# Ten elementwise instructions of each attention head move from GpSimd to VectorE and ScalarE

## The chip, the cores and the metric

The program runs on one core of a Trainium2 chip. A core has engines that run side by side, each through its own list of instructions in a fixed order: TensorE (PE in the profile, with PEld for its weight loads) does matmuls, VectorE (DVE) and GpSimd (POOL) do elementwise work on whole tiles, ScalarE (ACT) does functions of one input, and SyncE (SP) starts the loads of weights. An engine waits on semaphores for what another engine has to finish first. The metric is the device time of one execution in microseconds (us), lower is better.

## The reference

The model runs three blocks in turn over 512 tokens of width 1024. The change lies in the first two, which are alike and are called layers here. In each of them, eight groups of columns of one big projection feed two kinds of heads:

```python
for layer in range(DEPTH):            # DEPTH = 2
    h = rmsnorm(x, attn_norm[layer])
    proj = h @ w_in[layer]
    (a_q, a_k, a_v, b_q, b_ff, b_fb, b_i, b_g, gate_a, gate_b) = split_columns(proj)
    y_a = diff_attention(a_q, a_k, a_v, cos, sin, ...) @ w_a[layer]
    y_b = hgrn2_bidirectional(b_q, b_ff, b_fb, b_i, b_g, ...) @ w_b[layer]
    merged = sigmoid(gate_a) * y_a + sigmoid(gate_b) * y_b
    x = x + merged @ w_o[layer]
    ...                               # feed-forward part
```

`diff_attention` has 4 heads: queries and keys are rotated (a product with a cosine table plus a product of the shuffled tile with a sine table), and each head takes the difference of two softmaxes. `hgrn2_bidirectional` has 4 heads too: a linear recurrence over the tokens with a forget gate per channel, run forward and backward and added. Then follow a feed-forward part in each layer and a third block of another kind, which the change does not touch.

## The kernel before

Activations lie with channels on the 128 partitions and the 512 tokens along the free axis, so most tiles are 128x512 in float32. Every weight is loaded as `wraw`, and split into two parts, `whi` by ScalarE (L204) and `wlo` by VectorE (L205), and every projection is three matmuls for one product (L230 to L232). These matmuls are most of TensorE's work everywhere.

Each of the two layers has a heads part (about 88 to 310 us and 917 to 1140 us of the span), which goes through four heads, some 60 us each. A head h consists of

- `proj_rope` for the head's keys and queries: a projection, a shuffle (L650) and two products, one with the cosine table on VectorE (L651) and one with the sine table on GpSimd (L652, tile `rsh`), their sum (L653), and a split of the sum (`stack_split`) into `ak` or `aq` by ScalarE (L239) and VectorE (L243);
- `proj_h`: the projections of the recurrent head, its tiles in `H4` (forward keys, backward queries, forward queries, backward keys), and the sum of the two keys on GpSimd (L687, tile `hks`);
- `attn`, four blocks of queries: scores `at` (L249, L250), maxima (L715), exponentials `e` (L718), the two softmaxes' factors `arc` (L722, L723), their difference (L725), a transpose `tp` on TensorE (L728), and the product with the values (L734);
- `hgrn`, a scheme that doubles the block at each of eight levels (hh = 1, 2, 4, ... 128). A level copies the keys of the halves that it needs into `hKT` (L661, ScalarE), multiplies them with the queries on TensorE (L759; L767 at the last level), writes the result under a mask into `hWd` (L761, VectorE), and then multiplies the left halves (GpSimd from the second level on) and the right halves (VectorE) of all four tiles of `H4` in place with the decay `hT` (both L780). The next level's copy reads what these products wrote. After the last level come transposes of the keys (L793) and the last matmuls (L800 to L812);
- `head_norm`, with its power on GpSimd (L526).

`both` goes through `attn` and `hgrn` in turn, two levels for one block of queries, and the projections of the next head stand behind them in the program. A planner in the framework turns the program into one fixed list of instructions per engine before the launch: it goes through an estimated time, and each engine takes the earliest instruction of the program that the estimate calls ready. So TensorE's list has projections of the next head between the small matmuls of this one. In the run the lists are followed strictly, whatever the real times are.

Of the kernel before, what the change touches and what calls it, by code (L numbers as in the profile page):

```python
# [15 lines left out]
AF = mybir.ActivationFunctionType  # L16
ALU = mybir.AluOpType
# [54 lines left out]
def model_kernel(ctx: ExitStack, tc: tile.TileContext, I, O, dbg=None):  # L72
    nc = tc.nc
    V, A, P, PE = nc.vector, nc.scalar, nc.gpsimd, nc.tensor
# [548 lines left out]
    def heads(l, Win, nrm, oA, oB, op_, ah):  # L623
        Crs = ah.tile([128, 512], F32, name="Crs")
        Srs = ah.tile([128, 512], F32, name="Srs")
# [19 lines left out]
        def proj_rope(c0, tag):  # L645
            mark("proj_" + tag)
            ps = projA(Win, c0, 1, xs)[0]
            t1 = ah.tile([128, 512], F32, name="rt1", tag="rt1", bufs=1)
            sh = ah.tile([128, 512], F32, name="rsh", tag="rsh", bufs=1)
            V.stream_shuffle(out=sh, in_=ps, mask=[(i ^ 8) if i < 16 else i for i in range(32)])  # L650
            V.tensor_tensor(out=t1, in0=ps, in1=Crs, op=ALU.mult)  # L651
            P.tensor_tensor(out=sh, in0=sh, in1=Srs, op=ALU.mult)  # L652
            V.tensor_tensor(out=t1, in0=t1, in1=sh, op=ALU.add)  # L653
            dst = ah.tile([128, 2 if tag == "aq" else 4, 512], F32R, name=tag, tag=tag, bufs=2)
            stack_split(t1, dst)
            return dst
# [7 lines left out]
        def proj_h(h, rest=None):  # L664

            mark(f"projH{h}")
            ps = projA(Win, 1536 + h * 128, 1, xs)[0]
            q = ah.tile([128, 512], F32, name="hq", tag="hq", bufs=1)
            V.tensor_tensor(out=q, in0=ps, in1=rbc, op=ALU.mult)
            H4 = ah.tile([128, 4, 512], F32, name="H4", tag="H4", bufs=2)  # L670
            F2 = ah.tile([128, 2, 512], F32, name="F2", tag="F2", bufs=1)
            for d in range(2):
                ps = projA(Win, 2048 + d * 512 + h * 128, 1, xs)[0]
                z = ah.tile([128, 512], F32, name="hz", tag="hz", bufs=1)
                V.tensor_tensor(out=z, in0=ps, in1=rbc, op=ALU.mult)
                kk = H4[:, 0 if d == 0 else 3, :]
                A.activation(out=F2[:, d, :], in_=z, func=AF.Sigmoid)
                A.activation(out=kk, in_=z, func=AF.Sigmoid, scale=-1.0)
                if l == 1:
                    om = lbc[:, 1, d, h:h + 1]  # L680
                    V.tensor_scalar(out=F2[:, d, :], in0=F2[:, d, :], scalar1=om, scalar2=lbc[:, 0, d, h:h + 1],
                                    op0=ALU.mult, op1=ALU.add)
                    V.tensor_scalar(out=kk, in0=kk, scalar1=om, scalar2=None, op0=ALU.mult)
                V.tensor_tensor(out=H4[:, 2 if d == 0 else 1, :], in0=q, in1=F2[:, d, :], op=ALU.mult)
            KT = left_keys(H4, 1)
            ks = ah.tile([128, 512], F32, name="hks", tag="hks", bufs=1)
            P.tensor_tensor(out=ks, in0=H4[:, 0, :], in1=H4[:, 3, :], op=ALU.add)  # L687
            if rest is not None:
                rest()
                mark(f"projH{h}")  # L690
            dps = hg_ps()
            for b in range(4):
                sl = slice(b * 128, (b + 1) * 128)
                PE.matmul(out=dps[:, sl], lhsT=ks[:, sl], rhs=q[:, sl], start=True, stop=True)
            Wd = ah.tile([128, 4, 128], F32, name="hWd", tag="hWd", bufs=2)
            A.copy(out=Wd.rearrange("p a b -> p (a b)"), in_=dps)
            ps = projA(Win, 3584 + h * 128, 1, xs)[0]
            sg = op_.tile([128, 512], F32, name="hsg", tag="hsg", bufs=3)
            V.tensor_tensor(out=sg, in0=ps, in1=rbc, op=ALU.mult)
            A.activation(out=sg, in_=sg, func=AF.Sigmoid)  # L700
            return H4, F2, Wd, sg, KT
# [42 lines left out]
        def hgrn(h, H4, F2, Wd, sg, KT):  # L744
            T = F2
            W1 = ah.tile([128, 4, 128], F32, name="hW1", tag="hW1", bufs=1)
            kF, qB, qF, kB = (H4[:, i, :] for i in range(4))
            for li, hh in enumerate(LEVELS + [128]):
                nb = 512 // (2 * hh)
                mark(f"hgrn{h}")  # L750
                if hh <= 64:
                    ps = hg_ps()
                    n2 = 64 // hh

                    if li:
                        KT = left_keys(H4, hh)
                    for b in range(4):
                        sl = slice(b * 128, (b + 1) * 128)
                        PE.matmul(out=ps[:, sl].rearrange("p (n two h) -> p n two h", two=2, h=hh), lhsT=KT[:, sl],  # L759
                                  rhs=halves(H4, 1, 2, hh, b * 128, 128), start=True, stop=True)  # L760
                    V.copy_predicated(out=Wd, mask=cm[:, li, :].unsqueeze(1).to_broadcast([128, 4, 128]),  # L761
                                      data=ps.rearrange("p (a b) -> p a b", b=128))
                else:
                    ps = hg_ps()
                    for b in range(4):
                        sl, tl = slice(b * 128, (b + 1) * 128), slice((b ^ 1) * 128, (b ^ 1) * 128 + 128)
                        PE.matmul(out=ps[:, sl], lhsT=(kB if b & 1 else kF)[:, sl], rhs=(qB if b & 1 else qF)[:, tl],  # L767
                                  start=True, stop=True)
                    A.copy(out=W1.rearrange("p a b -> p (a b)"), in_=ps)
                Tv = T.rearrange("p d (n two) -> p d n two", two=2)  # L770
                for half in range(2):
                    v = H4[:, 2 * half:2 * half + 2, :].rearrange("p d (n two h) -> p d n two h", two=2, h=hh)
                    tgt = v[:, :, :, half, :]
                    mul = Tv[:, :, :, 1 - half]
                    eng = P if half == 0 and hh > 1 else V
                    if hh == 1:
                        eng.tensor_tensor(out=tgt.rearrange("p d n h -> p d (n h)"),
                                        in0=tgt.rearrange("p d n h -> p d (n h)"), in1=mul, op=ALU.mult)
                    else:
                        eng.tensor_tensor(out=tgt, in0=tgt, in1=mul.unsqueeze(3).to_broadcast([128, 2, nb, hh]),  # L780
                                        op=ALU.mult)
                if hh < 128:
                    T2 = ah.tile([128, 2, nb], F32, name="hT", tag=f"hT{hh}", bufs=1)
                    V.tensor_tensor(out=T2, in0=Tv[:, :, :, 0], in1=Tv[:, :, :, 1], op=ALU.mult)
                    T = T2
                yield

            mark(f"hgrn{h}")
            vs = slice(h * 128, (h + 1) * 128)
            ps = hg_ps()  # L790
            for b in range(4):
                sl = slice(b * 128, (b + 1) * 128)
                PE.transpose(ps[:, sl], (kB if b > 1 else kF)[:, sl], ident)  # L793
            KT = ah.tile([128, 512], F32, name="hKT", tag="hKT", bufs=1)
            A.copy(out=KT, in_=ps)
            yield
            mark(f"hgrn{h}")
            ps = hg_ps()
            for b in range(4):
                PE.matmul(out=ps[:, b // 2 * 128:b // 2 * 128 + 128], lhsT=KT[:, b * 128:(b + 1) * 128], rhs=vb[:, b, vs],  # L800
                          start=b % 2 == 0, stop=b % 2 == 1)
            St = ah.tile([128, 256], F32, name="hSt", tag="hSt", bufs=1)
            A.copy(out=St, in_=ps[:, 0:256])
            yield
            mark(f"hgrn{h}")
            o = hg_ps()
            for t in range(4):
                tl = slice(t * 128, (t + 1) * 128)
                PE.matmul(out=o[:, tl], lhsT=(qF if t > 1 else qB)[:, tl], rhs=St[:, 0:128] if t > 1 else St[:, 128:256],
                          start=True, stop=False)  # L810
                PE.matmul(out=o[:, tl], lhsT=W1[:, t ^ 1, :], rhs=vb[:, t ^ 1, vs], start=False, stop=False)
                PE.matmul(out=o[:, tl], lhsT=Wd[:, t, :], rhs=vb[:, t, vs], start=False, stop=True)  # L812
            A.copy(out=oB[:, h, :], in_=o)
            yield
# [478 lines left out]
    with ExitStack() as mst:  # L1293
        with ExitStack() as st:
# [63 lines left out]
            for i in range(4):  # L1358
# [3 lines left out]
                                in0=sg[:, i, :].rearrange("p (j n) -> p n j", j=C),  # L1362
# [274 lines left out]
```

## Time and profile before

| | |
|---|---|
| median of 3 runs | 2335.88 us (2334.86 to 2336.14) |
| the profiled execution's own time | 2336.02 us |
| its span, first to last instruction | 2334.2 us |
| TensorE busy | 2295.8 us (98%) |
| VectorE busy | 1354.9 us (58%) |
| ScalarE busy | 1028.1 us (44%) |
| GpSimd busy | 405.3 us (17%) |

The profiled execution's time is its span and 1.8 us around it. Busy time of TensorE is not the same as TensorE at its peak: its matmuls overlap in the records, a 128x512 one is shown with 0.39 us though the next one starts 0.23 us later.

### The profile page before, as it was taken

The numbers are of one execution on the slowest core, as the hardware profiler recorded it, in microseconds if no ns is written. First come the engines' busy times: TensorE is split into PE (matmuls) and PEld (weight loads), VectorE is DVE, ScalarE is ACT, GpSimd is POOL, SyncE is SP. The second block draws the span as 40 slices with busy tenths as digits, with TensorE's granted clock in tenths as the row PEclk, the third lists the DMA queues.
The fourth block names the chain that finished last, engine by engine and source line by source line (L and its number), as shares of the span: only waits on it lengthen the run. The fifth ranks groups of instructions, "written<-read, shape, count | busy, mean of one in ns | idle before, by whom it ended". The sixth has DMA issues, their size and how long they took to land. (4 is left out here: it accounts for less than half of the span.)

```text
span 2334.2 us, 30091 instructions
## 1 busy us (share of the span) xinstructions
PE 2295.8 (98%) x11175; PEld 1908.5 (82%) x11175; DVE 1354.9 (58%) x2368; ACT 1028.1 (44%) x1912; POOL 405.3 (17%) x728
## 2 busy tenths in 40 slices
PE   9999999999999999999999999999999999999998
PEld 7877788888888888787788888888877888888887
DVE  5777755644444556888556444444776875534344
ACT  6566644433233245666533333232457354534232
POOL 1122210070233201222100546020000102000002
PEclk9999999999999999999999999999999999999999
DMA  6211124333333342111143343332443533233331
GB/s 228 72 55 55 55 73 154 102 106 103 115 97 111 107 141 82 55 55 55 55 135 100 101 128 96 111 108 89 125 141 101 177 112 126 91 92 98 100 99 65
DMA packets 241267, 237.40 MB, mean 102 GB/s; under 512 B 18936, under 2 KB 215112, under 8 KB 241120
## 3 DMA queue, kind: packets, MB, share of 16 engines
q1 hardware_dynamic: 221728, 204.81, 28.9%
q10 hardware_dynamic: 15584, 21.33, 2.8%
q0 software_dynamic: 3808, 9.33, 1.3%
q8 instruction: 88, 1.44, 0.3%
q14 instruction: 59, 0.48, 0.1%
HBM read 216.42 MB, written 20.59 MB: 102 GB/s over the span
## 5 line engine op out<-in xcount | busy, mean ns | idle before, releaser
L205 DVE TENSOR_TENSOR wlo<-wraw,whi 128x512 fp32r<-128x512 f32 x736 | 521.0, 713 | 685.5 <-ACT whi L204 677.1
L204 ACT ACTIVATE whi<-wraw 128x512 fp32r<-128x512 f32 x736 | 459.2, 629 | 896.4 <-PE mm L231 675.1
L230 PE MATMUL mm<-xg,whi 128*128 128x512 f32 (+1 forms) x1736 | 677.8, 390 | 0.0
L231 PE MATMUL mm<-xg,whi 128*128 128x512 f32 (+1 forms) x1736 | 675.4, 389 | 0.4 <-DVE xg L1414 0.3
L232 PE MATMUL mm<-xg,wlo 128*128 128x512 f32 (+1 forms) x1736 | 672.8, 388 | 0.0
L230 PEld LDWEIGHTS mm<-xg,whi 128*128 128x128 f32 x1736 | 326.4, 188 | 65.5 <-issue 2.2
L232 PEld LDWEIGHTS mm<-xg,wlo 128*128 128x128 f32 x1736 | 326.3, 188 | 64.7 <-issue 0.8
L231 PEld LDWEIGHTS mm<-xg,whi 128*128 128x128 f32 x1736 | 326.6, 188 | 62.9 <-DVE xg L1414 0.8
L230 PE MATMUL mm<-a,whi 128*128 128x512 f32 x352 | 137.0, 389 | 0.0
L231 PE MATMUL mm<-a,whi 128*128 128x512 f32 x352 | 136.9, 389 | 0.0
L232 PE MATMUL mm<-a,wlo 128*128 128x512 f32 x352 | 136.9, 389 | 0.0
L780 POOL TENSOR_TENSOR H<-H,hT 128x512 f32<-128x512 f32 x56 | 67.2, 1199 | 217.5 <-PE hg L759 122.4
L230 PEld LDWEIGHTS mm<-a,whi 128*128 128x128 f32 x352 | 66.1, 188 | 14.0 <-issue 0.2
L231 PEld LDWEIGHTS mm<-a,whi 128*128 128x128 f32 x352 | 66.1, 188 | 13.7
L232 PEld LDWEIGHTS mm<-a,wlo 128*128 128x128 f32 x352 | 66.1, 188 | 13.6
L230 PE MATMUL mm<-mrg,whi 128*128 128x512 f32 (+1 forms) x208 | 75.9, 365 | 0.0
L231 PE MATMUL mm<-mrg,whi 128*128 128x512 f32 (+1 forms) x208 | 75.8, 365 | 0.0
L232 PE MATMUL mm<-mrg,wlo 128*128 128x512 f32 (+1 forms) x208 | 75.8, 364 | 0.0
L292 POOL TENSOR_TENSOR rr<-rc,mhalf 128x4 f32<-128x4 f32 (+1 forms) x5 | 9.2, 1837 | 365.4 <-DVE rc L290 365.4
L759 PEld LDWEIGHTS hg<-H,hKT 128*128 128x128 f32 x448 | 59.2, 191 | 12.7 <-ACT hKT L661 10.6
L759 PE MATMUL hg<-H,hKT 128*128 128x128 f32 x448 | 64.8, 288 | 3.7 <-ACT hKT L661 3.7
L1540 POOL TENSOR_TENSOR acc<-acc,gpb 128x512 f32<-128x512 f32 x4 | 5.5, 1412 | 322.4 <-ACT jk L1514 322.4
(524 smaller groups left out, 3806.6 us busy)
## 6 DMA issues: line engine op xcount, KB each, us to landing
wraw<-in_w_in_dram SPq DMA_DIRECT2D x118, 512.0 KB, 3.8
wraw<-in_w_gate_dram SPq DMA_DIRECT2D x44, 512.0 KB, 3.7
wraw<-in_w_up_dram SPq DMA_DIRECT2D x44, 512.0 KB, 3.8
wraw<-in_w_down_dram SPq DMA_DIRECT2D x40, 512.0 KB, 3.4
wraw<-in_w_ff_in_dram SPq DMA_DIRECT2D x32, 512.0 KB, 3.8
wraw<-in_w_ff_out_dram SPq DMA_DIRECT2D x32, 512.0 KB, 3.7
wraw<-in_w_o_dram SPq DMA_DIRECT2D x16, 512.0 KB, 3.3
xT<-xd SPq DMA_DIRECT2D x24, 256.0 KB, 5.7
```

The source lines that it names most:

```text
L204: A.activation(out=hi[:, :n], in_=raw, func=AF.Copy)
L205: V.tensor_tensor(out=lo[:, :n], in0=raw, in1=hi[:, :n], op=ALU.subtract)
L230: PE.matmul(out=ps, lhsT=ah, rhs=bh, start=first, stop=False)
L231: PE.matmul(out=ps, lhsT=ah, rhs=bl, start=False, stop=False)
L232: PE.matmul(out=ps, lhsT=al, rhs=bh, start=False, stop=last)
L292: P.tensor_tensor(out=r, in0=c, in1=mhalf[:, :n], op=ALU.pow)
L759: PE.matmul(out=ps[:, sl].rearrange("p (n two h) -> p n two h", two=2, h=hh), lhsT=KT[:, sl], rhs=halves(H4, 1, 2, hh, b * 128, 128), star ...
L780: eng.tensor_tensor(out=tgt, in0=tgt, in1=mul.unsqueeze(3).to_broadcast([128, 2, nb, hh]), op=ALU.mult)
L1540: P.tensor_tensor(out=acc[:, t, csl], in0=acc[:, t, csl], in1=gpb[:, csl], op=ALU.mult)
```

## The change

Of each head, ten instructions leave GpSimd: the two products with the sine table (queries and keys), the sum of keys, and the seven left-half products of the levels from hh = 2 to hh = 128. Nine of them become VectorE instructions of the same form. The tenth, the left half of the last level (hh = 128), becomes four ScalarE instructions, one for each of the two tiles and of the two blocks of 128 columns, which scale by a column of `hT`. GpSimd keeps its fills of `ak`, its powers and its own DMAs; no DMA, matmul or buffer is changed.

```diff
@@ proj_rope
             V.tensor_tensor(out=t1, in0=ps, in1=Crs, op=ALU.mult)
-            P.tensor_tensor(out=sh, in0=sh, in1=Srs, op=ALU.mult)
+            V.tensor_tensor(out=sh, in0=sh, in1=Srs, op=ALU.mult)
             V.tensor_tensor(out=t1, in0=t1, in1=sh, op=ALU.add)
@@ proj_h
-            P.tensor_tensor(out=ks, in0=H4[:, 0, :], in1=H4[:, 3, :], op=ALU.add)
+            V.tensor_tensor(out=ks, in0=H4[:, 0, :], in1=H4[:, 3, :], op=ALU.add)
@@ hgrn, in the loop over the two halves
-                    eng = P if half == 0 and hh > 1 else V
-                    if hh == 1:
-                        eng.tensor_tensor(out=tgt.rearrange("p d n h -> p d (n h)"),
+                    if hh == 128 and half == 0:
+                        for d in range(2):
+                            for n in range(nb):
+                                A.activation(out=tgt[:, d, n, :], in_=tgt[:, d, n, :], func=AF.Copy,
+                                             scale=mul[:, d, n:n + 1])
+                    elif hh == 1:
+                        V.tensor_tensor(out=tgt.rearrange("p d n h -> p d (n h)"),
                                         in0=tgt.rearrange("p d n h -> p d (n h)"), in1=mul, op=ALU.mult)
                     else:
-                        eng.tensor_tensor(out=tgt, in0=tgt, in1=mul.unsqueeze(3).to_broadcast([128, 2, nb, hh]),
+                        V.tensor_tensor(out=tgt, in0=tgt, in1=mul.unsqueeze(3).to_broadcast([128, 2, nb, hh]),
                                         op=ALU.mult)
```

## Rows read from the trace of the kernel before

**Rows 1.** The page: busy us of each engine, share, instructions

```profile
PE 2295.8 (98%) x11175; PEld 1908.5 (82%) x11175; DVE 1354.9 (58%) x2368; ACT 1028.1 (44%) x1912; POOL 405.3 (17%) x728
```

**Rows 2.** Busy us in 60 us: PE, PEld, DVE, ACT, POOL; granted clock, DMA share, GB/s

```profile
980.00:1040.00 60.00, 56.59 (x323) 47.21 (x322) 48.70 (x90) 37.53 (x79) 15.76 (x14) 1.00 0.18 53
```

**Rows 3.** Who PE waited for, whole span: us in total, times, longest

```profile
PE tp L728 <- DVE e L725: 10.4, 16, 1.1
PE at L249 <- DVE aq L243: 5.8, 7, 1.3
PE hg L759 <- ACT hKT L661: 3.7, 16, 0.3
...
PE hg L767 <- DVE H L780: 2.3, 8, 0.3
```

**Rows 4.** POOL's groups by form: count, busy us, mean ns

```profile
L780 POOL TENSOR_TENSOR H<-H,hT 128x512 f32<-128x512 f32 x56 | 67.2, 1199 | 217.5 <-PE hg L759 122.4 <-ACT e L718 58.7 <-ACT whi L204 20.7
L652 POOL TENSOR_TENSOR rsh<-rsh,Srs 128x512 f32<-128x512 f32 x16 | 20.7, 1294 | 57.4 <-DVE rsh L650 53.7 <-PE mm L231 3.7
...
L687 POOL TENSOR_TENSOR hks<-H 128x512 f32<-128x512 f32 x8 | 11.8, 1477 | 103.6 <-PE mm L231 56.3 <-ACT H L678 39.8 <-DVE H L683 7.4
```

**Rows 5.** DVE's groups by form, 60 to 310 us: count, busy us, mean ns

```profile
L205 DVE TENSOR_TENSOR wlo<-wraw,whi 128x512 fp32r<-128x512 f32 x52 | 41.1, 791 | 8.9 <-ACT whi L204 8.8
L780 DVE TENSOR_TENSOR H<-H,hT 128x512 f32<-128x512 f32 x28 | 27.4, 979 | 1.0 <-PE hg L767 0.7
...
L784 DVE TENSOR_TENSOR hT<-F 128x512 f32<-128x512 f32 x4 | 6.1, 1523 | 0.0
...
L723 DVE TENSOR_TENSOR arc<-arc,nlam 128x1 f32<-128x1 f32 x16 | 5.8, 365 | 0.4
...
L777 DVE TENSOR_TENSOR H<-H,F 128x512 f32<-128x512 f32 x8 | 5.1, 684 | 0.0
```

**Rows 6.** Line L723 in the whole span: shortest, median, longest in ns

```profile
L723 DVE TENSOR_TENSOR arc<-arc,nlam x32: 148/159/996, 96.9 to 1125.6; 128x1 f32<-128x1 f32 x32
```

**Rows 7.** Timeline, second query block of the first head: start us, duration us

```profile
102.13 1.16 POOL L780 TENSOR_TENSOR H<-H,hT 128x512 f32<-128x512 f32 x1 [2.65 <-ACT e L718]
...
102.32 0.99 DVE L723 TENSOR_TENSOR arc<-arc,nlam 128x1 f32<-128x1 f32 x1
...
103.84 0.73 DVE L725 SCALAR_TENSOR_TENSOR e<-e,arc 128x512 f32<-128x512 f32 x1
...
104.72 0.63 PE L728 MATMUL tp<-ident,e 128*128 128x128 f32 x4 [1.10 <-DVE e L725]
```

**Rows 8.** Timelines of DVE and POOL, rotation of the first head's queries

```profile
86.87 1.35 DVE L205 TENSOR_TENSOR wlo<-wraw,whi 128x512 fp32r<-128x512 f32 x1
88.14 0.68 DVE L653 TENSOR_TENSOR rt<-rt,rsh 128x512 f32<-128x512 f32 x1
...
86.38 1.30 POOL L652 TENSOR_TENSOR rsh<-rsh,Srs 128x512 f32<-128x512 f32 x1 [3.61 <-DVE rsh L650]
```

**Rows 9.** Timeline, one level of the recurrence in the first head

```profile
107.21 0.73 DVE L761 COPY_PREDICATED hWd<-cm,hg 128x512 f32<-128x512 uint8 x1 [0.17 <-PE hg L759]
107.31 1.10 POOL L780 TENSOR_TENSOR H<-H,hT 128x512 f32<-128x512 f32 x1 [4.02 <-ACT e L718]
107.84 1.12 DVE L780 TENSOR_TENSOR H<-H,hT 128x512 f32<-128x512 f32 x1
...
109.05 0.62 ACT L661 COPY hKT<-H 128x512 f32<-128x512 f32 x1 [1.80 <-DVE amx L716]
```

**Rows 10.** Timeline, last level of the first layer's last head

```profile
300.29 0.59 ACT L769 COPY hW<-hg 128x512 f32<-128x512 f32 x1 [1.52 <-PE hg L767]
...
300.40 1.48 POOL L780 TENSOR_TENSOR H<-H,hT 128x512 f32<-128x512 f32 x1 [1.97 <-PE hg L767]
...
301.94 0.66 PE L793 MATMUL hg<-ident,H 128*128 128x128 f32 x4 [0.36 <-POOL H L780]
```

**Rows 11.** ScalarE's 128x128 instructions of line L522: shortest, median, longest in ns

```profile
L522 ACT ACTIVATE hjk<-oA x32: 294/298/313, 125.4 to 1134.3; 128x128 f32<-128x128 f32 x32
```

## The prediction

> **What bounds the kernel now.** I read the page first, for which engine is full: TensorE, 98% busy, VectorE second with 58% [rows 1]. An average says little about a change that touches two parts of the span, so the busy times by stretch come next, for the heads alone. In 60 us of the second layer's heads TensorE is busy for 56.6, VectorE for 48.7, ScalarE for 37.5, GpSimd for 15.8, at a granted clock of 1.00, the 2.4 GHz level, so the clock has nothing to give [rows 2]. TensorE sets the time here too, and what the change can win or lose is how long TensorE stands still. The table of waits, read for TensorE, says for what: VectorE's `e`, VectorE's `aq`, ScalarE's `hKT` and the right-half product, 10.4 + 5.8 + 3.7 + 2.3 = 22.2 us [rows 3], nearly all of them in the heads. That is the ceiling, about 1% of the span. None of these waits names GpSimd. The question is thus whether GpSimd's ten instructions per head make VectorE late, and this is read from single instructions: the groups by form and the timeline.
>
> **What GpSimd costs VectorE now.** On VectorE a 128x512 product takes 684 ns where GpSimd rests (the first level's) and 979 on average in the later levels, where GpSimd multiplies the other half [rows 5]. `arc`, one column wide, takes 159 ns as a rule and 996 at worst [rows 6]. The timeline shows such a case: GpSimd's product runs from 102.13 to 103.29, and `arc`, begun at 102.32, ends at 103.31, right behind it [rows 7]. A `wlo` that meets the sine product takes 1.35 us instead of 0.68 [rows 8]. So a VectorE instruction that meets a GpSimd product stands still until that is done. Summed over the first layer, against 684 ns (159 for `arc`): L780 28 x 295 = 8.3 us, `wlo` 52 x 107 = 5.6, `hT` 4 x 839 = 3.4, `arc` 16 x 206 = 3.3 [rows 5], 20.6 us, and for both layers, which run the same code, an estimate of 41 us. This is time that VectorE gets back.
>
> **What VectorE pays.** Nine products in each of 8 heads: 72 x 684 ns = 49 us, 6.2 us a head. GpSimd is rid of 67.2 + 20.7 + 11.8 = 99.7 us [rows 4], which ends nothing. VectorE's balance is thus 49 - 41 = +8 us in 480, about 1 us per head, beside 11.3 us in which it idles now [rows 2]. On VectorE's load the change is a draw, so it is decided by which instructions come earlier and which later.
>
> The page SBUF — State Buffer of the Trainium skill (Who interferes with whom) says that VectorE's second read port is GpSimd's too, and that whichever starts first holds it for its whole instruction. The `arc` of [rows 7] agrees. Taken literally over all 99.7 us the rule would give VectorE 99.7 - 49 = 51 us back, not a debt of 8; the rows give 41 because VectorE is often idle, or reads PSUM, while GpSimd multiplies. On that reading VectorE would be free wherever `e` and `aq` want it, so both terms below would stand at their upper ends and the sum would be -6.7 - 4.2 + 2.0 + 0.4 = -8.5 us. I go by the rows.
>
> **Earlier: `e`.** In the second query block of each head `arc` waits out a GpSimd product, 996 - 159 = 0.84 us, then come the mask write and L725, and TensorE's transposes wait 1.10 us for it [rows 7]. The mean of `arc`, 365 ns, is that of 4 such cases in 16 [rows 5], one per head, and 8 x 1.1 = 8.8 of the 10.4 us stand there. If VectorE is free, 0.84 x 8 = 6.7 us go; nothing goes if a product that is now VectorE's own stands in front of `arc` instead. The planner takes the earlier instruction of the program, and the softmax of this block stands ahead of this level's products, so a product comes first only when it is already running. Near the upper end: **-5.6 us** (0.7 a head).
>
> **Earlier: `aq`.** The sine product ends at 87.68, but the sum L653 begins at 88.14, behind the `wlo` that was held until then [rows 8]. With the sine product on VectorE at 86.87, done at 87.55, the sum can follow there, if the planner does not put `wlo` in between; the sum is the earlier instruction. That is up to 0.6 us per head, in 7 of 8 places where TensorE waits 0.83 us on average [rows 3]: at most 7 x 0.6 = 4.2 us, at least 0. As the order favours the sum, I take three quarters: **-3.1 us**.
>
> **Later: the levels.** Now: mask write at 107.21, right half held from 107.84 to 108.96, next copy at 109.05 [rows 9]. After: mask write, left half from 107.84, right half 0.60 later (records back to back overlap by 0.08, as `wlo` and the sum do in [rows 8]), ending at 109.12: 0.16 us later per level. There is no room on VectorE to hide it in; what hides it is the next head's projections between the small matmuls, which the planner places by its estimate. Where TensorE waits already, there is no cover: 16 waits for `hKT` and 8 for the last level's product [rows 3], the latter later by about 0.3, as 1.28 us for the pair stands against 0.98 on average for a held right half [rows 5]. At worst 16 x 0.16 + 8 x 0.3 = 5.0 us. At best nothing, or a gain of 2.3 when the products go ahead of the mask write, which the last level's matmuls do not need. The planner sees the serial pair and can place projections ahead; a bit under half of the worst: **+2.0 us**.
>
> **The last level on ScalarE.** Four 128x128 instructions of 295 ns or so [rows 11], 1.18 us, behind the copy `hW`: 300.88 + 1.18 = 302.06, where GpSimd ended at 301.88 [rows 10]. In the last head of a layer nothing covers that: 0.2 us twice. If the copy of `oA` (about 0.6 us, as `hW`) goes first, 0.8 twice. Elsewhere projections stand ready. **+0.4 us** (0 to 1.6). ScalarE, 37.5 us of 60 [rows 2], carries 1.2 more. What queues behind the four is the transposed keys' copy, which waits for the same products.
>
> **At nothing:** the sum of keys is needed one rotation later, and 0.68 on VectorE replaces 1.48 on GpSimd [rows 4] that held `hT` for 0.84; its cover is the projections of keys and queries, without which it would cost 8 x 0.68 = 5 us. GpSimd's fills and powers can only start earlier. No DMA is moved past any queue.
>
> **Sum:** -5.6 - 3.1 + 2.0 + 0.4 = -6.3 us. The profiled execution took 2336.02 us (span 2334.2, and 1.8 around it), which is 0.14 above the median of the runs. So 2329.7 us, 0.27% below the median. The bounds together: -6.7 - 4.2 - 2.3 = -13.2 (2322.8) and +5.0 + 1.6 = +6.6 (2342.6).
>
> **The rivals.**
> *Hidden anyway (0.28).* VectorE frees `arc`, but the planner, whose estimate now has three times 0.7 us in a row there, reorders both lists, and a product or a `wlo` of 0.68 us stands where the held one stood. For it: VectorE is left only 10 us of idle time a head. Against: the same wait of 1.1 us stands in the same place of every head, so it comes from one cause. With `e` and `aq` at a quarter: -1.7 -1.0 + 2.0 + 0.4 = -0.3, 2335.7 us.
> *The serial pair decides (0.17), slower.* At every level the next copy comes 0.16 us later, and at a bad moment a full 0.68. If projections run short at the levels, TensorE pays for each: 8 x 6 x 0.16 + 8 x 0.3 = 10.1 us, with `e` won back by half (-3.4): +6.7, 2342.7 us. It decides from 0.1 us per level on that TensorE really waits, if `e` and `aq` give nothing. Against it: TensorE waits for `hKT` at only 2 of 7 levels, for 0.2 us each [rows 3].
> *The load decides (0.05), slower.* If little of the 41 us comes back, VectorE stands at 48.7 + 6.2 = 54.9 of 60 us in a head [rows 2], and the 16 waits for `e` and 7 for `aq` each grow by half a product, 23 x 0.34 = 7.8 us: 2343.8 us. The Trainium skill's Perfetto Trace Analysis (Optimizing Scalar/DVE Operations) speaks for giving a saturated VectorE's work away, even to GpSimd, so against this change; the same passage doubts it where the two share a port, and the held `arc` agrees with the doubt.
>
> **How the numbers follow.** The forecast has 0.50, with its own range of 2322.8 to 2332. The other half lies at no change and above. A measurement of this kernel can tell some 0.2%, 4.7 us, from no change; the forecast passes that by 1.6 us. Faster 0.50, same 0.28, slower 0.22 (the last two rivals). The range reaches from 2322 to 2343, the outer bounds; what lies outside is half of the first slow rival and most of the second, and a few in a hundred below.
>
> **What would show it.** Right: `arc` and the H products never above 0.2 and 0.75 us; TensorE's wait for `e` at 3 to 5 us in all; that for `aq` at 2 to 4; `hKT` waits somewhat up. VectorE's busy time within 10 us of before, GpSimd's some 100 lower. Wrong would be a wait for `e` as long as now, with a product or `wlo` ahead of `arc` on VectorE, or waits for `hKT` of several tenths at many levels. A list of TensorE that comes out ordered otherwise far from the heads could also move the time by a few us in either direction, which no row here can price.

## The result and the profile after

The changed kernel takes 2307.28 us (median of 4 runs, 2306.7 to 2307.52) against 2335.76 us: a ratio of 0.9879, 95% interval 0.9867 to 0.989. It is 28.5 us faster, where 6.2 were forecast, and below the lower end of the range. The direction and the cause that the prediction gave hold; the size does not.

The page of the kernel after, busy us of each engine:

```profile
span 2305.4 us, 30070 instructions
...
PE 2288.1 (99%) x11175; PEld 1908.5 (83%) x11175; DVE 1346.3 (58%) x2440; ACT 1033.7 (45%) x1944; POOL 306.6 (13%) x648
```

The span fell by 28.8 us and TensorE's busy time by 7.7, though its 11175 matmuls are the same [rows 1]. So its idle time by the records fell by only 21.1 us, from 38.4 to 17.3. The 7.7 us are about the part that the records hide: a 128x512 matmul is shown with 0.39 us, but the next can start after 0.23. Where one does wait, the last 0.16 us of the record before it already are lost time, and the page calls them busy.

Stretch by stretch, in the same 60 us of the span as before [rows 2] (columns: PE, PEld, DVE, ACT, POOL; clock, DMA share, GB/s):

```profile
980.00:1040.00 60.00, 60.00 (x348) 50.81 (x348) 51.81 (x107) 40.74 (x89) 3.33 (x4) 1.00 0.21 62
```

TensorE has no gap left there and runs 348 matmuls where 323 ran; the granted clock is 1.00 in both. The first and the last scores matmul (L249) started at 90.6 and 1119.5 us before and start at 89.8 and 1092.7 now: 26.0 of the 28.5 us lie between them, in the two heads parts and what stands between.

Who TensorE waited for in the kernel after, the top of the table (us in total, times, longest):

```profile
PE mm L230 <- DVE gA L556: 2.8, 2, 1.5
PE mi L300 <- POOL rr L292: 2.1, 1, 2.1
PE mi L365 <- DVE half L463: 1.8, 1, 1.8
PE hg L797 <- DVE H L784: 1.1, 1, 1.1
```

All four rows of [rows 3] are gone, `hKT` and the last level's product too. What is left was there before or stands outside the heads, except for 1.1 us behind the last level of one head.

VectorE's groups by form in the first heads part, kernel after (count, busy us, mean ns, idle before), the last row ScalarE's:

```profile
L205 DVE TENSOR_TENSOR wlo<-wraw,whi 128x512 fp32r<-128x512 f32 x58 | 39.5, 684 | 7.6 <-ACT whi L204 7.2 <-PE mm L232 0.3
L784 DVE TENSOR_TENSOR H<-H,hT 128x512 f32<-128x512 f32 x52 | 33.7, 680 | 4.1 <-PE hg L767 4.1
L788 DVE TENSOR_TENSOR hT<-F 128x512 f32<-128x512 f32 x4 | 2.7, 684 | 0.0
...
L723 DVE TENSOR_TENSOR arc<-arc,nlam 128x1 f32<-128x1 f32 x16 | 2.4, 153 | 0.2
...
L778 ACT ACTIVATE H<-H,hT 128x128 f32<-128x128 f32 x16 | 5.6, 392 | 0.3 <-PE hg L767 0.3
```

Every VectorE instruction that was long at times [rows 5] now has its undisturbed duration: `wlo` 684 ns for 791, the level products 680 for 979, `hT` 684 for 1523, `arc` 153 for 365. The timeline of VectorE at the second query block of the first head, kernel after (start us, duration us), is the place of [rows 7]:

```profile
101.42 0.73 DVE L761 COPY_PREDICATED hWd<-cm,hg 128x512 f32<-128x512 uint8 x1 [1.40 <-PE hg L759]
102.05 0.15 DVE L722 RECIPROCAL arc<-als 128x2 f32<-128x2 f32 x1
102.12 0.67 DVE L784 TENSOR_TENSOR H<-H,hT 128x512 f32<-128x512 f32 x1
102.71 0.15 DVE L723 TENSOR_TENSOR arc<-arc,nlam 128x1 f32<-128x1 f32 x1
102.78 0.68 DVE L784 TENSOR_TENSOR H<-H,hT 128x512 f32<-128x512 f32 x1
103.38 0.74 DVE L725 SCALAR_TENSOR_TENSOR e<-e,arc 128x512 f32<-128x512 f32 x1
```

Two products of VectorE's own now stand around `arc`. From the start of `arc` to the start of L725 pass 0.67 us instead of 1.52. TensorE's transposes come at 104.27 with no wait: TensorE's list has projections up to there.

### The profile page after: what moved, and what is told of

The parts are those of the page before. It is cut to its first block, busy times and chain, and to the rows that moved or that the text cites. A ratio compares the mean times of both kernels' runs of the same rounds, so it can differ in the third digit from the quotient of the medians.

```text
span 2305.4 us, 30070 instructions
## 1 busy us (share of the span) xinstructions
PE 2288.1 (99%) x11175; PEld 1908.5 (83%) x11175; DVE 1346.3 (58%) x2440; ACT 1033.7 (45%) x1944; POOL 306.6 (13%) x648
## 5 line engine op out<-in xcount | busy, mean ns | idle before, releaser
L205 DVE TENSOR_TENSOR wlo<-wraw,whi 128x512 fp32r<-128x512 f32 x736 | 511.6, 700 | 673.9 <-ACT whi L204 669.4
L526 POOL TENSOR_TENSOR rr<-hss,mhalf 128x4 f32<-128x4 f32 x16 | 17.5, 1096 | 519.4 <-DVE hss L524 519.4
L784 DVE TENSOR_TENSOR H<-H,hT 128x512 f32<-128x512 f32 x104 | 67.5, 680 | 5.2 <-PE hg L767 5.2
L759 PE MATMUL hg<-H,hKT 128*128 128x128 f32 x448 | 65.5, 287 | 0.0
L759 PEld LDWEIGHTS hg<-H,hKT 128*128 128x128 f32 x448 | 60.0, 191 | 5.5 <-ACT hKT L661 3.1
```

The costliest lines, as they stand in the source:

```text
L205: V.tensor_tensor(out=lo[:, :n], in0=raw, in1=hi[:, :n], op=ALU.subtract)
L526: P.tensor_tensor(out=r, in0=ssq, in1=mhalf[:, 0:4], op=ALU.pow)
L784: V.tensor_tensor(out=tgt, in0=tgt, in1=mul.unsqueeze(3).to_broadcast([128, 2, nb, hh]), op=ALU.mult)
```

## The experiments

Medians of before beside these runs were 2335.79 us (the first four), 2336.04 (e5 to e8) and 2335.23 (the rest). "Lists" below are the instructions of an engine in order, compared by name without line numbers.

**e1_fill: GpSimd's instructions stay, but read nothing.** Before, with each of GpSimd's ten instructions as two fills of the same tile; the ten products and sums are not computed.

```diff
-            P.tensor_tensor(out=sh, in0=sh, in1=Srs, op=ALU.mult)
+            for _ in range(2):
+                P.memset(sh, 0.5)
```

(and the same for `ks` and for the left half `tgt`.)

> The kernel before, with each of GpSimd's ten instructions per head replaced by two GpSimd fills of the same tile with a constant (so these products and sums are not computed): GpSimd still writes at the same place of the chain for about 1.05 us, but reads nothing. The lists of TensorE and ScalarE are those of before, instruction for instruction, VectorE's too but for two places. Theory 'held' (VectorE's two-input instructions stand still while GpSimd reads, which the planned lists do not allow for): 2306 to 2314 us, L723 never above 0.2 us, right-half products 0.68. Theory 'list' (the new lists, which put more projections ahead of the small matmuls, are what wins): 2330 to 2336, as the lists are the old ones. Theory 'slow GpSimd' (its 1.1 to 1.5 us in the chain of the levels): 2328 to 2336.

Measured: 2303.76 us, ratio 0.9865 (0.985 to 0.988). TensorE's and ScalarE's lists are those of before, VectorE's differs in four rows. Groups of e1_fill, whole span (shortest/median/longest ns) and, in the second row, 60 to 310 us; then its waits of TensorE from the top:

```profile
L783 POOL MEMSET H<- x112: 525/527/603, 97.1 to 1099.3; 128x512 f32 x112
L785 DVE TENSOR_TENSOR H<-H,hT 128x512 f32<-128x512 f32 x28 | 19.0, 680 | 1.0 <-PE hg L769 0.7
L725 DVE TENSOR_TENSOR arc<-arc,nlam x32: 149/159/161, 96.0 to 1094.0; 128x1 f32<-128x1 f32 x32
```

```profile
PE mi L300 <- POOL rr L292: 2.1, 1, 2.1
PE mi L365 <- DVE half L463: 1.8, 1, 1.8
PE mm L230 <- DVE gA L556: 1.7, 2, 1.3
PE hg L1287 <- DVE hi L935: 1.3, 1, 1.3
```

GpSimd writes the rotated tiles and the left halves at the places of before, 1.05 us a pair, next to the 1.2 of its product. Only the fills of `ks`, which have no input to wait for, ran 40 us and more ahead. VectorE is no longer held (680 ns for 979; `arc` 161 at the longest), and with the order of before all four waits of [rows 3] are gone. So the gain needs neither the new order nor a faster second engine; it comes with what GpSimd no longer reads. Removing the holds alone is worth 32.0 us, 2.2 more than the range of 'held' allowed.

TensorE's list is the same in both runs, so the two traces can be laid over each other matmul by matmul. From one start to the next, TensorE loses 11.9 us less at the transposes (L728 of before), 9.6 less at the scores (L249, L250), 6.6 less at L759 and 2.6 less at L767. That is 30.7 of the 32.4 us by which the span is shorter.

**e2_ghost_products and e3_ghost_fills: the holds put back.** After, with one GpSimd instruction for each of six levels (48 in all) whose result nobody uses; it reads what the mask write has just written, so it runs beside the two products of the level.

```diff
+                if 1 < hh < 128:
+                    gh = ah.tile([128, 512], F32, name="gh", tag="gh", bufs=1)
+                    wdf = Wd.rearrange("p a b -> p (a b)")
+                    P.tensor_tensor(out=gh, in0=wdf, in1=wdf, op=ALU.mult)   # e2
+                    P.memset(gh, 0.0)                                        # e3, in its place
```

> The changed kernel, with 48 extra GpSimd products (one per level from hh = 2 to 64, both inputs the masked tile hWd, result not used) that start behind the mask write, when VectorE does the level's two products. All lists of TensorE, VectorE and ScalarE are those of the changed kernel. 'Held': the waits come back in part, 0.3 to 0.5 us per ghost that meets VectorE: 2314 to 2328 us. 'List': the lists cover it, 2306 to 2311. 'Slow GpSimd': nothing waits for the ghosts' results, 2306 to 2309.

> The control for the run with ghost products: the same extra tile, written by a GpSimd fill at each level, which reads nothing. Lists as in the changed kernel. All theories: 2306 to 2310 us.

Measured: e2 2338.39 us, ratio 1.0009 (1.0 to 1.0019); e3 2308.2 us, 0.9881 (0.9867 to 0.9896). All lists but GpSimd's are those of after in both. The 48 products cost 30.2 us against the fills, 0.63 us each: the whole gain is gone, more than any theory had put there. TensorE's waits in e2, then groups of e2 and its timeline of VectorE and GpSimd:

```profile
PE hg L759 <- ACT hKT L661: 9.9, 18, 0.9
PE tp L728 <- DVE e L725: 7.7, 10, 0.8
PE hg L767 <- DVE H L788: 5.5, 8, 0.8
```

```profile
L788 DVE TENSOR_TENSOR H<-H,hT 128x512 f32<-128x512 f32 x52 | 47.3, 940 | 4.4 <-PE hg L767 4.4
L723 DVE TENSOR_TENSOR arc<-arc,nlam x32: 147/159/999, 96.1 to 1127.1; 128x1 f32<-128x1 f32 x32
L773 POOL TENSOR_TENSOR gh<-hWd x48: 1292/1392/1993, 98.3 to 1133.3; 128x512 f32<-128x512 f32 x48
```

```profile
102.90 0.67 DVE L788 TENSOR_TENSOR H<-H,hT 128x512 f32<-128x512 f32 x1
...
103.02 1.45 POOL L773 TENSOR_TENSOR gh<-hWd 128x512 f32<-128x512 f32 x1 [3.39 <-DVE arc L722]
...
103.49 1.00 DVE L723 TENSOR_TENSOR arc<-arc,nlam 128x1 f32<-128x1 f32 x1
```

Three of the four waits are back, 23.1 us by the table. `arc`, begun at 103.49, ends at 104.49, right behind GpSimd's instruction (104.47). As a control e3 has a gap: its fills have no inputs and ran ahead, as its group shows, so it holds the lists and the extra tile fixed but not the place. That fills at the place do not hold VectorE is e1's to show.

```profile
L772 POOL MEMSET gh<- x48: 515/527/544, 3.1 to 844.3; 128x512 f32 x48
```

**e9_ghost_early and e10_ghost_copies: what a hold depends on.** As e2, but e9's product reads the keys' copy and so runs during the level's matmuls, and e10's instruction has one input.

```diff
+                    P.tensor_tensor(out=gh, in0=KT, in1=KT, op=ALU.mult)                # e9
+                    P.tensor_copy(out=gh, in_=Wd.rearrange("p a b -> p (a b)"))         # e10
```

> As the run with ghost products, but the 48 ghosts read the copied keys hKT, so they run while TensorE does the level's matmuls, ahead of VectorE's mask write and two products, not beside them. Lists as in the changed kernel. 'Held' says that a ghost costs only where a two-input VectorE instruction stands beside it; VectorE then does maxima, wlo and softmax factors, fewer of which gate TensorE: 2309 to 2322 us. If mere GpSimd reading beside any VectorE work costs, as much as the other ghosts: 2333 to 2340.

> As the run with ghost products (behind the mask write), but each ghost is a GpSimd copy, one input instead of two. Lists as in the changed kernel. If reading as such holds VectorE: 0.4 to 0.7 us per ghost again, 2322 to 2340 us. If only GpSimd's second input does: 2307 to 2312.

Measured: e9 2315.26 us, 0.9913 (0.99 to 0.9927), 7.1 us over e3, 0.15 for each product, in the range of 'held'. e10 2323.6 us, 0.995 (0.9936 to 0.9963), 15.4 us over e3, 0.32 for each copy; the time lies in the range for reading as such, the price of one copy below it. Groups of e9 (VectorE's from 60 to 310 us, GpSimd's of the whole span), and of e10 in the same way:

```profile
L787 DVE TENSOR_TENSOR H<-H,hT 128x512 f32<-128x512 f32 x52 | 33.8, 680 | 4.1 <-PE hg L767 4.1
...
L723 DVE TENSOR_TENSOR arc<-arc,nlam 128x1 f32<-128x1 f32 x16 | 7.0, 439 | 0.2
...
L772 POOL TENSOR_TENSOR gh<-hKT 128x512 f32<-128x512 f32 x48 | 56.2, 1172 | 374.5 <-ACT hKT L661 374.5
```

```profile
L787 DVE TENSOR_TENSOR H<-H,hT 128x512 f32<-128x512 f32 x52 | 41.7, 833 | 4.4 <-PE hg L767 4.4
L772 POOL COPY gh<-hWd x48: 871/982/1048, 98.4 to 1119.3; 128x512 f32<-128x512 f32 x48
```

A GpSimd product that is somewhat shorter costs a quarter when it falls where the level's products are not yet due: they are unheld (680 ns), and it is mostly `arc` that still meets it (439 ns on average). One input is enough to hold (833 for 680); the copy is shorter, and so is the hold.

**e4 to e7: the parts alone.** e4 is after with sine product and key sum back on GpSimd; e5 is before with the sine product on VectorE, e6 with the key sum, e7 with the last level's left half on ScalarE.

```diff
-            P.tensor_tensor(out=sh, in0=sh, in1=Srs, op=ALU.mult)
+            V.tensor_tensor(out=sh, in0=sh, in1=Srs, op=ALU.mult)       # e5; e4 the other way
-            P.tensor_tensor(out=ks, in0=H4[:, 0, :], in1=H4[:, 3, :], op=ALU.add)
+            V.tensor_tensor(out=ks, in0=H4[:, 0, :], in1=H4[:, 3, :], op=ALU.add)   # e6; e4 the other way
+                    if hh == 128 and half == 0:                         # e7, the rest as before
+                        ... A.activation(... scale=mul[:, d, n:n + 1])
```

> The change without two of its parts: the sine products and the sum of keys stay on GpSimd, the left halves go to VectorE and ScalarE. TensorE's list is that of the changed kernel. 'Held': 16 sine products and 8 sums hold VectorE for 0.7 to 1.1 us each in front of the first scores: 2309 to 2315 us, TensorE's wait for aq back at 2 to 5 us. 'List': 2306 to 2309. 'Slow GpSimd': the sine product takes 1.3 instead of 0.7, so aq is later by up to 0.6 at 8 places: 2308 to 2312.

> One part alone: only the two sine products of each head go to VectorE, everything else as before. TensorE's list is that of before. 'Held': the table of waits had 5.8 us for aq, and start to start some 7 us; these go, the waits for e and hKT stay: 2326 to 2331 us. 'List' is no longer open after the fill run (old lists, 2303.8 us); by it nothing would change: 2334 to 2337.

> One part alone: only the sum of keys goes to VectorE. TensorE's list is that of before. 'Held': it held hT for 0.84 us eight times, far ahead of the level that needs it: 2333 to 2336 us.

> One part alone: only the last level's left half goes, to ScalarE; the six other levels, the sine products and the sum stay on GpSimd. 'Held': the last level's product meets only the next head's products: 2332 to 2337 us. TensorE's list changes in part, which adds a few us of doubt in either direction.

| | us | ratio (95%) | against before |
|---|---|---|---|
| e4, levels | 2309.34 | 0.9889 (0.9872 to 0.9905) | -26.4 |
| e5, sine | 2334.8 | 0.9995 (0.9986 to 1.0004) | -1.2 |
| e6, key sum | 2333.62 | 0.999 (0.998 to 0.9999) | -2.4 |
| e7, last level | 2336.7 | 1.0004 (0.9994 to 1.0013) | +0.7 |

TensorE's list in e4 is that of after, in e5 and e6 that of before. The levels, with the new TensorE list that comes with them, are nearly all of it. e4's time lies at the lower end of 'held', where 'slow GpSimd' allows it too, but its sign is missing: 2 to 5 us of wait for `aq` were expected, and 0.3 are there. e6 and e7 lie in their ranges. e5 missed its range. Its timeline of VectorE at a rotation and its waits of TensorE:

```profile
145.59 0.68 DVE L652 TENSOR_TENSOR rsh<-rsh,Srs 128x512 f32<-128x512 f32 x1
146.19 0.68 DVE L205 TENSOR_TENSOR wlo<-wraw,whi 128x512 fp32r<-128x512 f32 x1
146.79 0.69 DVE L653 TENSOR_TENSOR rt<-rt,rsh 128x512 f32<-128x512 f32 x1
```

```profile
PE tp L728 <- DVE e L725: 10.6, 16, 1.1
PE at L249 <- DVE aq L243: 4.1, 5, 1.1
```

The planner put a `wlo` between the sine product and the sum. The sum starts 1.20 us after the sine product began. Before, it started 1.27 us after the held `wlo` had begun at the same place in VectorE's list [rows 8], so nearly nothing is won. In e6 `hT` is no longer held (group by form, 60 to 310 us):

```profile
L784 DVE TENSOR_TENSOR hT<-F 128x512 f32<-128x512 f32 x4 | 2.7, 685 | 0.0
```

**e8_all_ten_vector and e11_mask_behind: variants of after.** e8 leaves the ScalarE branch out, so VectorE has all ten. e11 puts the mask write of a level (up to hh = 64) behind its two products, so that what the next copy waits for comes earlier.

```diff
-                    if hh == 128 and half == 0:            # e8
-                        ... A.activation(...)
-                V.copy_predicated(...)                     # e11: moved behind the loop over the halves
```

> As the changed kernel, but the last level's left half on VectorE as well, so all ten are there. 'Held': GpSimd reads nothing in either: 2305 to 2310 us, against 2307.3. If ScalarE's four short ones are what helps at the end of a head, 2310 to 2314.

> The changed kernel with the mask write behind the level's two products in the program, so the next copy of keys can start 0.6 to 0.7 us earlier at each level. The lists change. If the serial pair still costs TensorE something (the fill run, without it, took 3.5 us less), 2303 to 2307 us; if the projections cover it, 2306 to 2309.

Measured: e8 2308.33 us, 0.9881 (0.9866 to 0.9896); e11 2308.13 us, 0.9883 (0.9869 to 0.9896). By the intervals neither can be told from after. Products that need not stand behind the mask write (0.73 us) give nothing, so the pair in a row on VectorE is covered.

**e12_more_to_vector: the same idea elsewhere.** After, and outside the heads 16 more GpSimd products on VectorE: eight beside the scan of the third block and eight at the residuals.

```diff
-            mul(tq3, xi, Rs, P)
+            mul(tq3, xi, Rs)
-            mul(tq4, xr, Rs, P)
+            mul(tq4, xr, Rs)
-                    (P if m % 2 else V).tensor_tensor(out=ym, in0=ym, in1=bc, op=ALU.mult)
+                    V.tensor_tensor(out=ym, in0=ym, in1=bc, op=ALU.mult)
```

> The changed kernel, and in the third block GpSimd's 8 products of the scan and 4 of the residual (two halves each) go to VectorE too. TensorE waits there for VectorE's gA and hi, 3.1 us in all. 'Held' says that a hold is part of this: 2303 to 2306 us. If VectorE is simply full there: 2306 to 2311.

Measured: 2300.25 us, 0.9849 (0.9835 to 0.9862), 7 us below after, below both ranges and the best of all. The scan and a stretch around it (columns as above), first in after, then in e12:

```profile
L1272 DVE TENSOR_TENSOR_SCAN xi<-ma,xi x4: 2306/2314/2318, 1778.1 to 1828.4; 128x512 f32<-128x512 f32 x4
1640.00:1820.00 180.00, 176.61 (x865) 138.27 (x864) 128.75 (x285) 91.87 (x197) 11.06 (x11) 1.00 0.48 144
```

```profile
L1272 DVE TENSOR_TENSOR_SCAN xi<-ma,xi x4: 1199/1218/1222, 1779.0 to 1826.2; 128x512 f32<-128x512 f32 x4
1640.00:1820.00 180.00, 178.98 (x885) 140.79 (x884) 131.31 (x294) 94.72 (x202) 2.49 (x6) 1.00 0.50 147
```

This scan was held to nearly twice its length; VectorE took on 16 products and its busy time fell from 1346.3 to 1344.8 us. Only about 3 of the 7 us are won around the scan, where the waits for `gA` fall from 2.8 to 0.3 us. About 4 are won at and right behind one place near the residuals, where TensorE waits 2.1 us in after for a GpSimd instruction, the power `rr`. There it is GpSimd that stands still (timeline of after, VectorE and GpSimd):

```profile
1943.46 3.69 DVE L205 TENSOR_TENSOR wlo<-wraw,whi 128x512 fp32r<-128x512 f32 x6
1943.62 4.08 POOL L292 TENSOR_TENSOR rr<-rc,mhalf 128x2 f32<-128x2 f32 x1 [7.23 <-DVE rc L290]
```

Beside six `wlo` in a row the power takes 4.08 us; in e12, where VectorE does something else after one `wlo`, it takes 1.07. No run changes this place alone, so that the row of `wlo` is the reason is not shown.

## Why the prediction was right in kind and wrong in size

**Right: what GpSimd's instructions do to VectorE.** The prediction read from `arc` and the two durations of the products that VectorE stands still behind GpSimd. e1 takes only the reading away and the waits go; e2 puts only reading instructions back and they return. The Trainium skill's SBUF — State Buffer (Who interferes with whom) lets a VectorE instruction with two inputs from SBUF collide with a GpSimd instruction that reads SBUF, not with one that only writes; the runs agree: 680 ns beside fills (e1), 940 beside products (e2), 833 beside copies (e10).

**Right: VectorE's load is a draw.** 8.6 us less busy (1354.9 to 1346.3), where 8 us more were worked out and 10 either way allowed. e1, with the holds gone and no work added, has 1310.9: the holds were 44 us, near the 41 estimated. "The load decides" is refuted.

**Wrong: "That is the ceiling, about 1% of the span".** The 22.2 us of [rows 3] count from the end of the matmul's record, which outlasts the time to the next start by 0.16 us. With 47 waits that is 22.2 + 47 x 0.16 = 29.7 us that the waits really cost, an estimate that the 32.0 of e1 and the 28.5 of after lie around. Laid over e1, the four waits cost 30.7 us from start to start. In e2 one wait can be followed: the transposes start 1.16 us after the projection before them where 0.23 would do, and the table gives 0.78.

**Wrong: "Later: the levels", +2.0 us.** This is the largest error, and it has the wrong sign. The prediction took the waits for `hKT` and for the last level's product as places without cover, where a serial pair costs more. They were holds themselves: the right half on VectorE took 979 ns on average and so ended 0.3 us late (0.44 in [rows 9]), and it is what `hKT`'s copy and L767 wait for. 3.7 + 2.3 us by the table could be won there, 9.2 from start to start (6.6 + 2.6), and e1 wins them with the old lists. After, the pair does end later (2.04 us from the mask write's start in the timeline above, with `arc` in between, 1.75 in [rows 9]), but TensorE's list has projections ahead, and no wait for `hKT` is left. e11 bears out the cover. "The serial pair decides" is refuted.

**Wrong: `e`, -5.6 us.** All 16 waits went, 10.4 us by the table and 11.9 from start to start, not only the 0.84 us of `arc` in one block of each head. The prediction followed one instruction and took its hold for the bound (6.7 us). The timeline of before has the other holds, in the first head:

```profile
98.85 1.18 DVE L780 TENSOR_TENSOR H<-H,hT 128x512 f32<-128x512 f32 x1
...
111.56 1.10 DVE L780 TENSOR_TENSOR H<-H,hT 128x512 f32<-128x512 f32 x1
112.58 0.74 DVE L725 SCALAR_TENSOR_TENSOR e<-e,arc 128x512 f32<-128x512 f32 x1
```

The first is a right half of 1.18 us instead of 0.68, ahead of the second block. ScalarE's copy of the keys waits 0.24 us for VectorE there, and the exponentials and `arc` come behind that copy, so `arc` is late by as much before its own hold of 0.84 us begins. The second stands right ahead of L725 in the third block, 0.42 us too long, where TensorE waits about 0.2 us by the table; the eight short waits are those of this block, one in each head.

**Wrong: `aq`, -3.1 us, by the sum right behind the sine product.** The wait is gone, 5.8 us by the table and 9.6 from start to start in e1. But the step as put does not happen: `wlo` stands between the two in e5, where 4.1 us of the wait stay, and in after. Nor is the time lost in the queries' rotation. In the last head, from the shuffle of the queries to the first scores pass 4.76 us before and 4.77 in e4, where 0.3 us of the wait are left in all heads together. It is the keys' rotation, one earlier, that starts late. Before, its shuffle begins at 1088.28, 2.3 us after the keys' projection has ended, and behind `hT`, which the sum of keys holds:

```profile
1084.81 1.79 DVE L784 TENSOR_TENSOR hT<-F 128x512 f32<-128x512 f32 x1
```

In e1, with the order of before and `hT` unheld, it begins 1.2 us after the projection, and the wait is gone. In e4 this `hT` is still held, but in six of the eight heads TensorE's new list has 32 to 36 other matmuls between the recurrent head's projections and that of the keys, where before has none. VectorE comes to `hT` 5.1 us ahead of the projection's end instead of 1.2, and the shuffle begins 0.8 us after it. So either is nearly enough, the hold taken away or the new order that covers it; after has both.

**The small terms.** The last level on ScalarE, +0.4: e7 (+0.7 against GpSimd) has this sign; in e8 ScalarE is 1.0 us cheaper than VectorE would be, and neither can be told from zero. Its four instructions average 392 ns, not 295. The key sum was put at nothing because its result is needed one rotation later; alone it gave 2.4 us (its interval ends at 0.9999). What counted was not its result but its hold: `hT` went from 1523 ns to 685, and TensorE's wait for `aq` from 5.8 to 4.2 us.

**Hidden anyway.** Refuted for the whole change, but it is what happens to the sine product alone (e5).

**Open.** e1 is 3.5 us faster than after; 1.1 us of that is the wait behind the last level of one head, which e1 does not have. e11 shows that the order of mask write and products is not it; whether it is the 49 us of products that VectorE carries, or the list, was not tried.

## What to carry to other kernels

When a fixed order was planned from undisturbed durations, look first for one and the same instruction with two durations, and for what the other engine runs meanwhile: each of these holds is a delay that the order has no cover for, while added work of known length can be planned around. So try to give the work that collides to the engine that suffers from it, even if it looks fuller: here VectorE took nine products per head and was less busy. Count a wait from start to start of the matmuls around it, and before trusting the cause put the collision back alone, with instructions whose result nobody reads.

## What the runs showed of the hardware

- A GpSimd fill of 128x512 (527 ns) does not slow a two-input VectorE instruction beside it (680 ns in e1). A GpSimd copy with one input does (833 ns in e10), and so does a product (940 in e2).
- The price of a GpSimd instruction that reads is set by what VectorE has to do meanwhile, more than by its length: 0.15 us of the program's time in e9 (1172 ns long on average), 0.32 for the copies of e10 (median 982 ns), 0.63 in e2 (median 1392 ns).
- VectorE's scan of 128x512 is held too: 2.31 us beside GpSimd's products, 1.22 without.
- GpSimd can stand still as well: a power of 128x2 took 4.08 us beside six of VectorE's two-input instructions in a row, and 1.07 in e12.
